# Removing the pauses inside the barrier norms of a two-layer hybrid encoder step

## The chip, the core and the metric

The kernel runs on one core of a Trainium2 chip. The metric is the device time of one execution in microseconds (us). The kernel before takes 2740.53 us, the median of three runs (2738.47 to 2742.73).

## What is computed

One inference step of a two-layer encoder over 640 positions: 512 of a new stream and 8 running streams of 16. Cut to what matters here, a layer is

```
h = rmsnorm(x, g_pre_mix);  u = h @ w_in
...   three branches (convolution, attention, state space) from u, merged by gates
x = x + rmsnorm(merged @ w_out, g_post_mix)
f = rmsnorm(x, g_pre_ffn) @ w_gate_up
f = (silu(f[..., :D_FF]) * f[..., D_FF:]) @ w_down
x = x + rmsnorm(f, g_post_ffn)
rmsnorm(x, g) = x * rsqrt(mean(x * x) + EPS) * g
```

The model width is 1024, the feed-forward width 2816. Two norms stand next to each other at each of a layer's two barriers: the norm after `w_out` or `w_down`, whose result is added to x, and the norm ahead of the next projection, which needs all 1024 channels of that x.

## The kernel before, in words

**Layout.** Activations lie transposed: 8 tiles of 128 channels by 640 positions. The positions are cut in two halves, half 0 of 256 and half 1 of 384 columns (`HALF`). A *unit* (`Unit`) is one 128x128-column strip of a weight matrix for all its inputs. Each weight and each activation is split in two parts (`split`: a rounded part on ScalarE, the rest on VectorE), and three matmuls per pair make up for the precision, so a unit with 8 input tiles is 24 matmuls per half. Its sum lies in a PSUM buffer of the pool `psg`, of which there are four (tile names `pg`). After the matmuls an evacuation function reads the buffer and frees it.

**A norm.** `sq_acc` (line 414) squares each evacuated tile on ScalarE (tile `sq`, the first of them `acc`) and VectorE adds it to `acc`. `colsum` (line 184) sums over the channels with matmuls against ones (tile `cs`), `rsqrt` (line 191) is nine small VectorE instructions (last one `ry`), `bcast` (line 208) spreads the root over 128 partitions with matmuls (tile `rb`). In `postnorm` (line 424) the eight tiles of x are loaded again (`xl`), VectorE multiplies the eight tiles by `rb` and gain and adds `xl`, `squares` (line 390) squares the eight results on ScalarE (`psq`) and adds them in seven steps on VectorE, and the results go to DRAM. `prenorm` (line 398) then takes `colsum`, `rsqrt`, `bcast` again, writes eight tiles `ht` on VectorE, and splits them into the parts `hh` (ScalarE) and `hl` (VectorE) that the next units read.

**Order of the work.** The code is written as one list of actions. `barrier` and `add_halves` (lines 336 and 325) write a stage's units like this: half 0 of all eight units of `w_out` (or `w_down`), then half 1 of all eight; beside half 1 runs the norm of half 0. Then come twelve units of the next stage with half 0, and beside them runs the norm of half 1; then the halves 1 of these. "Beside" is a generator: after each half unit, `pump` (line 283) gives each lane a credit, and one credit lets a norm be written up to its next `yield`. So the yields say after how many units which part of a norm is written into the program. In the units of 8 input tiles a lane gets one step per half unit, with a step saved up from before, so two after the first; in the 7-input units of `w_down` it gets 0.875.

**What written order decides.** The tile framework then places each instruction on the queue of its engine at build time: as early as what it needs is ready in the framework's own estimate, and among several that are ready the one that is written first. So written order is no order of execution. But each pool hands out its buffers strictly in the order in which the code first writes them. In the program of the kernel before, none of the 904 tiles of the pool `hf` is first written out of that order. `hf` (line 87) has 11 buffers, and `acc`, `sq`, `xl`, `psq`, `ht`, and the feed-forward evacuation's `ft` and `fg` all come from it.

**Evacuations.** `wout` (line 1301) copies the PSUM buffer and squares it from PSUM (`sq`), so the buffer is free after both. `down` (line 1337) adds the buffer to `dn` on VectorE and squares `dn`, so its buffer is free without an `hf` tile. `gu` (line 1322) writes, for a gate unit, tanh into `ft` (ScalarE), then `fg` (VectorE); for the up unit behind it `fg` is multiplied by the buffer and split. `ev_lora` (line 540) copies the buffer and squares it from PSUM into `acc` or `sq`.

Of the kernel before, what the change touches and what calls it, by code (L numbers as in the profile page):

```python
# [17 lines left out]
D_MODEL, SEQ, DEPTH, NB, DS, PAST = 1024, 512, 2, 8, 16, 256  # L18
# [53 lines left out]
BY = 2  # L72
# [4 lines left out]
def emit(tc, ctx, I, O):  # L77
# [27 lines left out]
    def hf(w, s="h", dt=F32):  # L105
        return hpool.tile([P, w], dt, tag="hf", name=nm(s))
# [7 lines left out]
    def tiny(shape, s="t", dt=F32):  # L114
        return tpool.tile(shape, dt, tag="t", name=nm(s))

    def psb(shape, s="pb"):
        return psb_.tile(shape, F32, tag="pb", name=nm(s))

    def mm(ps, l, r, a, b):  # L120
        nc.tensor.matmul(ps, l, r, start=a, stop=b)  # L121
# [14 lines left out]
    def tt(eng, o, a, b, op):  # L136
        eng.tensor_tensor(o, a, b, op=op)  # L137

    def stt(o, a, s, b, op0, op1):
        return V.scalar_tensor_tensor(o, a, s, b, op0=op0, op1=op1)  # L140
# [10 lines left out]
    def split(hi, lo, src, eng=None):  # L151
        nc.scalar.copy(hi, src)  # L152
        tt(eng or V, lo, src, hi.bitcast(F32), ALU.subtract)
# [30 lines left out]
    def colsum(sq, n):  # L184

        ps = psb([P, 24], "cs")
        for j in range(n):
            mm(ps[:, j:j + 1], sq[:, j * P:(j + 1) * P], C["ones"], True, True)
        return ps

    def rsqrt(ps, n, scale, post=1.0):

        v, q = ps[:, 8:8 + n], ps[:, 16:16 + n]
        s, r, t, y = (tiny([P, 8], x)[:, :n] for x in ("rs", "rr", "rt", "ry"))
        a = V.tensor_scalar(v, ps[:, :n], scale / post ** 2, EPS / post ** 2, op0=ALU.mult, op1=ALU.add)
        for i in tap.values():
            tc.add_manual_dep(a.ins, i.ins.name, behind)
        V.tensor_scalar(s.bitcast(I32), v.bitcast(I32), 0.5, float(0x1fbb4f2e), op0=ALU.mult, op1=ALU.add)
        V.reciprocal(r, s)
        tt(V, q, v, r, ALU.mult)  # L200
        tt(V, t, q, s, ALU.add)
        V.reciprocal(r, t)
        tt(V, q, v, r, ALU.mult)
        stt(t, t, 0.25 * HERON ** 2, q, ALU.mult, ALU.add)
        root.append(V.reciprocal(y, t))
        return y

    def bcast(y, n):
        rb = psb([P, n * P], "rb")
        for j in range(n):  # L210
            mm(rb[:, j * P:(j + 1) * P], y[:, j:j + 1].broadcast_to([P, P]), C["ident2"], True, True)
        return rb
# [144 lines left out]
    def layer(l):  # L357
# [21 lines left out]
        def par(n, j):  # L379
            o = _PK[n][0]  # L380
            return L["pk"][:, o + j:o + j + 1]


        def new_h():
            L["h"] = [tuple(blk([P, NT], t, F32R) for t in ("hh", "hl")) for _ in range(8)]
# [4 lines left out]
        def squares(xs, half):  # L390
            r = [hf(HW[half], "psq") for _ in range(8)]
            for k in range(8):
                act(r[k], xs[k][:, HALF[half]], AF.Square)
            for a, b in ((0, 1), (2, 3), (4, 5), (6, 7), (0, 2), (4, 6), (0, 4)):
                tt(V, r[a], r[a], r[b], ALU.add)
            return r[0]

        def prenorm(xs, sq, half, gname, ps=None):
            c, w, n = HALF[half], HW[half], HCH[half]
            if ps is None:  # L400
                ps = colsum(sq, n)
            yield
            y = rsqrt(ps, n, 1.0 / D_MODEL)
            yield
            rb = bcast(y, n)
            for k in range(8):
                tmp = hf(w, "ht")
                stt(tmp, xs[k][:, c], par(gname, k), rb, ALU.mult, ALU.mult)
                hh, hl = L["h"][k]
                split(hh[:, c], hl[:, c], tmp)  # L410
            yield
# [12 lines left out]
        def postnorm(key, tiles, half, gname, src, dst, sq=True):  # L424

            c, n, w = HALF[half], HCH[half], HW[half]
            yield
            ps = colsum(L.pop(("sq", key, half)), n)
            xs = []
            for k in range(8):  # L430
                xs.append(hf(w, "xl"))
                dma(xs[k], src[k][:, c])
            yield
            rb = bcast(rsqrt(ps, n, 1.0 / D_MODEL), n)
            for k in range(8):
                t = tiles[k][:, c]
                stt(t, t, par(gname, k), rb, ALU.mult, ALU.mult)
                tt(V, t, t, xs[k], ALU.add)
            r = squares(tiles, half) if sq else None
            for k in range(8):  # L440
                dma(dst[k][:, c], tiles[k][:, c])
            for _ in range(BY):
                yield
            return r


# [865 lines left out]
        def bar_mix(half):  # L1312
            sq = yield from postnorm("mo", L["mo"], half, "g_post_mix", xin, xd)
            if half == 0:
                new_h()
            yield
            yield from prenorm(L["mo"], sq, half, "g_pre_ffn")


# [34 lines left out]
        def bar_ffn(half):  # L1354
            sq = yield from postnorm("dn", L["dn"], half, "g_post_ffn", xd, O["y"] if last else xd, not last)
            if not last:
                nxt = layers[l + 1]
                if half == 0:
                    nxt["load_params"]()
                    nxt["new_h"]()  # L1360
                yield
                yield from nxt["prenorm"](L["dn"], sq, half, "g_pre_mix")

        def start():
# [3 lines left out]
        def first_norm(half):  # L1368
            sq = ps = None
            if half == 0:  # L1370

                ps = psb([P, 24], "cs")
                r = [hf(HW[0], "psq") for _ in range(8)]
                for k in range(8):
                    act(r[k], x0[k][:, HALF[0]], AF.Square)
                    if k % 2 == 0:
                        continue
                    tt(V, r[k], r[k], r[k - 1], ALU.add)
                    for j in range(HCH[0]):

                        mm(ps[:, j:j + 1], r[k][:, j * P:(j + 1) * P], C["ones"], k == 1 and j == 0, k == 7 and j == HCH[0] - 1)
            else:
                for _ in range(Y1):
                    yield
                sq = squares(x0, 1)
                yield
            yield from prenorm(x0, sq, half, "g_pre_mix", ps)

        def schedule():
# [36 lines left out]
            add_units([mix_ssm(m) for m in range(8)])  # L1426
            us = [u for j in range(6) for u in gu(j)]
            barrier([wout(m) for m in range(8)], KEEP_W[1], bar_mix, us[-KEEP_W[2]])
            add_halves(us, KEEP_W[2])
            for g in range(3):  # L1430
# [5 lines left out]
            if last:  # L1436

                add_halves([down(2, m) for m in range(8)], KEEP_W[3], 1, lambda: lanes["bar"].append(bar_ffn(1)))
                add_hook(lambda: lanes["bar2"].append(bar_ffn(0)))
                add_hook(lambda: (flush("bar"), flush("bar2")))  # L1440

        xin = I["x"] if l == 0 else xd
        return dict(schedule=schedule, start=start, load_params=load_params, new_h=new_h, prenorm=prenorm, bar_ffn=bar_ffn, down=down)

    layers = [layer(l) for l in range(DEPTH)]
# [181 lines left out]
```

## Time and profile before

| what | value |
|---|---|
| median of three runs | 2740.53 us |
| the profiled execution's own time | 2738.25 us |
| its span, first to last instruction | 2736.4 us |
| TensorE busy | 2647.6 us, 97% |
| VectorE, ScalarE, GpSimd busy | 1557.0, 1092.8, 810.7 us |
| mean granted TensorE clock | 0.988 |

TensorE's idle time is 88.8 us in all. The four barriers stand at 820 to 910 us (layer 0, `w_out`), 1310 to 1420 us (`w_down` of layer 0 into layer 1), 2195 to 2295 us (layer 1, `w_out`) and 2700 us to the end. Busy times of a stage say how full an engine is there; what a wait costs is read from TensorE's waits in that stage.

### The profile page before, as it was taken

The numbers are of one execution on the slowest core, as the hardware profiler recorded it, in microseconds if no ns is written. First come the engines' busy times: TensorE is split into PE (matmuls) and PEld (weight loads), VectorE is DVE, ScalarE is ACT, GpSimd is POOL, SyncE is SP. The second block draws the span as 40 slices with busy tenths as digits, with TensorE's granted clock in tenths as the row PEclk, the third lists the DMA queues.
The fourth block names the chain that finished last, engine by engine and source line by source line (L and its number), as shares of the span: only waits on it lengthen the run. The fifth ranks groups of instructions, "written<-read, shape, count | busy, mean of one in ns | idle before, by whom it ended". The sixth has DMA issues, their size and how long they took to land. (4 is left out here: it accounts for less than half of the span.)

```text
span 2736.4 us, 47467 instructions
## 1 busy us (share of the span) xinstructions
PE 2647.6 (97%) x17652; PEld 2556.6 (93%) x17652; DVE 1557.0 (57%) x3382; ACT 1092.8 (40%) x2437; POOL 810.7 (30%) x796
## 2 busy tenths in 40 slices
PE   7999999999999899999999899999999998999997
PEld 7999898889999899999999898989999998999997
DVE  6364759576566632333665648677656666323336
ACT  5535454434325432222445354544433344322222
POOL 5554555554420000000156544645544200000000
PEclk9999999999999999999999999999999999999999
DMA  6453244543734432222454432453436443222224
GB/s 185 147 159 102 75 135 111 156 131 119 239 121 137 149 93 74 70 82 72 139 166 158 129 98 87 128 143 120 145 110 230 133 159 120 86 77 70 78 74 131
DMA packets 248536, 337.81 MB, mean 123 GB/s; under 512 B 52464, under 2 KB 139056, under 8 KB 248304
## 3 DMA queue, kind: packets, MB, share of 16 engines
q1 hardware_dynamic: 246720, 333.75, 39.2%
q8 instruction: 139, 2.28, 0.3%
q10 hardware_dynamic: 1584, 1.02, 0.1%
q14 instruction: 93, 0.76, 0.1%
HBM read 268.73 MB, written 65.94 MB: 122 GB/s over the span
## 5 line engine op out<-in xcount | busy, mean ns | idle before, releaser
L121 PE MATMUL pg<-hh,wh 128*128 128x256 f32 (+1 forms) x3296 | 1048.4, 319 | 25.6 <-DVE fg L140 18.2
L121 PE MATMUL pg<-hl,wh 128*128 128x256 f32 (+1 forms) x3296 | 1035.1, 314 | 4.6 <-DVE hl L137 4.6
L121 PE MATMUL pg<-hh,wl 128*128 128x256 f32 (+1 forms) x3296 | 1029.2, 313 | 0.0
L137 POOL TENSOR_TENSOR wl<-raw,wh 128x512 fp32r<-128x512 f32 (+2 forms) x364 | 506.8, 1398 | 1158.5 <-ACT wh L152 1106.3
L152 ACT CAST wh<-raw 128x512 fp32r<-128x512 f32 (+1 forms) x696 | 423.7, 610 | 846.7 <-PE pg L121 737.9
L121 PEld LDWEIGHTS pg<-hh,wh 128*128 128x128 f32 x3296 | 627.3, 190 | 37.7 <-DVE fg L140 18.6
L121 PEld LDWEIGHTS pg<-hl,wh 128*128 128x128 f32 x3296 | 627.6, 191 | 13.8 <-DVE hl L137 5.3
L121 PEld LDWEIGHTS pg<-hh,wl 128*128 128x128 f32 x3296 | 627.0, 190 | 5.6 <-issue 3.9
L137 DVE TENSOR_TENSOR wl<-raw,wh 128x512 fp32r<-128x512 f32 x332 | 224.3, 677 | 338.6 <-ACT wh L152 337.0
L121 PE MATMUL pg<-fh,wh 128*128 128x256 f32 (+1 forms) x648 | 200.6, 310 | 0.0
L121 PE MATMUL pg<-fl,wh 128*128 128x256 f32 (+1 forms) x648 | 200.1, 309 | 0.0
L121 PE MATMUL pg<-fh,wl 128*128 128x256 f32 (+1 forms) x648 | 200.0, 309 | 0.0
L140 DVE SCALAR_TENSOR_TENSOR cv<-pp,pk,cv 128x512 f32<-128x512 f32 x184 | 158.8, 863 | 2.7 <-POOL cv L137 2.7
L121 PEld LDWEIGHTS pg<-fh,wh 128*128 128x128 f32 x648 | 122.0, 188 | 0.0
L121 PEld LDWEIGHTS pg<-fl,wh 128*128 128x128 f32 x648 | 122.0, 188 | 0.0
L121 PEld LDWEIGHTS pg<-fh,wl 128*128 128x128 f32 x648 | 121.9, 188 | 0.0
L140 DVE SCALAR_TENSOR_TENSOR sa<-pd,pk,sa 128x664 f32<-128x664 f32 x96 | 106.6, 1110 | 16.9 <-ACT sa L996 16.3
L137 POOL TENSOR_TENSOR cv<-cv,cvt 128x640 f32<-128x640 f32 x56 | 89.8, 1603 | 74.4 <-ACT cvt L907 66.2
L140 DVE SCALAR_TENSOR_TENSOR cv<-sp,pk,cv 128x128 f32<-128x128 f32 x184 | 94.8, 515 | 0.0
L137 DVE TENSOR_TENSOR fg<-fg,pg 128x256 f32<-128x256 f32 (+1 forms) x88 | 42.6, 486 | 83.5 <-PE pg L121 83.2
L152 ACT CAST fh<-fg 128x256 fp32r<-128x256 f32 (+1 forms) x88 | 40.3, 460 | 111.3 <-DVE fg L137 108.3
L137 DVE TENSOR_TENSOR acc<-acc,sq 128x256 f32<-128x256 f32 (+1 forms) x96 | 59.8, 625 | 37.4 <-ACT sq L421 35.9
(307 smaller groups left out, 4411.7 us busy)
## 6 DMA issues: line engine op xcount, KB each, us to landing
raw<-in_w_in SPq DMA_DIRECT2D x284, 256.0 KB, 2.9
raw<-in_w_gu SPq DMA_DIRECT2D x208, 256.0 KB, 2.7
raw<-in_w_down SPq DMA_DIRECT2D x72, 256.0 KB, 2.7
raw<-in_w_mix SPq DMA_DIRECT2D x64, 256.0 KB, 3.0
ma<-gd SPq DMA_DIRECT2D x48, 320.0 KB, 4.7
raw<-in_w_out SPq DMA_DIRECT2D x48, 256.0 KB, 2.7
gd<-gs SPq DMA_DIRECT2D x48, 192.0 KB, 2.2
hb<-in_state_ssm SPq DMA_DIRECT2D x64, 128.0 KB, 3.2
```

What stands on the lines that cost most here:

```text
L121: nc.tensor.matmul(ps, l, r, start=a, stop=b)
L137: eng.tensor_tensor(o, a, b, op=op)
L140: return V.scalar_tensor_tensor(o, a, s, b, op0=op0, op1=op1)
L152: nc.scalar.copy(hi, src)
```

## The change

In `prenorm` the two pauses between the column sums and the root and between the root and the broadcast go, in `postnorm` the one between the loads and the root; behind `postnorm` one pause is left of two, and the pause between the two norms goes at both kinds of barrier. The instructions, their number and their tiles stay as they are. With `BY = 2`, written steps per norm pair go from 8 to 3: one empty step, then everything of `postnorm`, then everything of `prenorm`.

```diff
@@ prenorm
             if ps is None:
                 ps = colsum(sq, n)
-            yield
-            y = rsqrt(ps, n, 1.0 / D_MODEL)
-            yield
-            rb = bcast(y, n)
+            rb = bcast(rsqrt(ps, n, 1.0 / D_MODEL), n)
             for k in range(8):
@@ postnorm
                 dma(xs[k], src[k][:, c])
-            yield
             rb = bcast(rsqrt(ps, n, 1.0 / D_MODEL), n)
@@ postnorm
                 dma(dst[k][:, c], tiles[k][:, c])
-            for _ in range(BY):
-                yield
+            yield
             return r
@@ bar_mix
                 new_h()
-            yield
             yield from prenorm(L["mo"], sq, half, "g_pre_ffn")
@@ bar_ffn
                     nxt["new_h"]()
-                yield
                 yield from nxt["prenorm"](L["dn"], sq, half, "g_pre_mix")
```

## Rows read from the trace of the kernel before

**Rows 1.** The page, part 1: busy time, share and instructions of each engine.
```profile
PE 2647.6 (97%) x17652; PEld 2556.6 (93%) x17652; DVE 1557.0 (57%) x3382; ACT 1092.8 (40%) x2437; POOL 810.7 (30%) x796
```

**Rows 2.** Busy time by stage: length, PE, PEld, DVE, ACT, POOL (instructions), clock, DMA.
```profile
820.00:910.00 90.00, 79.46 (x571) 79.06 (x570) 62.49 (x147) 44.45 (x99) 0.00 (x0) 0.96 0.52 167
910.00:1310.00 400.00, 400.00 (x2692) 400.00 (x2691) 156.14 (x291) 119.88 (x230) 0.00 (x0) 1.00 0.26 80
1310.00:1420.00 110.00, 103.48 (x727) 102.66 (x726) 82.50 (x195) 55.16 (x120) 41.65 (x31) 0.94 0.54 168
...
2195.00:2295.00 100.00, 89.47 (x627) 89.07 (x626) 74.16 (x181) 47.90 (x106) 0.00 (x0) 0.95 0.46 150
```

**Rows 3.** TensorE's waits, barriers one, two, three: waited for, total us, times, longest.
```profile
PE pg L121 <- DVE fg L140: 9.1, 1, 9.1
PE pg L121 <- DVE hl L137: 1.5, 1, 1.5
...
PE rb L121 <- DVE ry L205: 2.5, 1, 2.5
PE pg L121 <- ACT sq L421: 2.4, 1, 2.4
PE pg L121 <- DVE hl L137: 1.7, 1, 1.7
...
PE pg L121 <- DVE hl L137: 1.4, 1, 1.4
```

**Rows 4.** Timeline of the first barrier, TensorE: start, us, instruction [idle before, releaser].
```profile
870.81 0.50 PE L121 MATMUL cs<-c_ones,psq 128*128 128x1 f32 x4
...
877.23 0.60 PE L121 MATMUL rb<-c_ident,ry 128*128 128x128 f32 x4
...
909.45 0.58 PE L121 MATMUL pg<-hh,wh 128*128 128x256 f32 x1 [9.08 <-DVE fg L140]
```

**Rows 5.** Timeline of the first barrier, ScalarE.
```profile
862.99 1.32 ACT L393 ACTIVATE psq<-mo 128x256 f32<-128x256 f32 x4
864.21 0.86 ACT L421 ACTIVATE sq<-pg 128x384 f32<-128x384 f32 x2
...
905.15 2.17 ACT L393 ACTIVATE psq<-mo 128x384 f32<-128x384 f32 x5
907.22 0.63 ACT L1325 ACTIVATE ft<-pg 128x256 f32<-128x256 f32 x2
...
920.89 0.38 ACT L1325 ACTIVATE ft<-pg 128x256 f32<-128x256 f32 x1 [0.93 <-PE pg L121]
```

**Rows 6.** Timeline of the first barrier, VectorE.
```profile
873.37 0.17 DVE L205 RECIPROCAL ry<-rt 128x2 f32<-128x2 f32 x1
...
911.25 0.55 DVE L137 TENSOR_TENSOR psq<-psq,psq 128x384 f32<-128x384 f32 x1
...
922.60 4.29 DVE L140 SCALAR_TENSOR_TENSOR ht<-mo,pk,rb 128x384 f32<-128x384 f32 x8 [1.73 <-PE rb L121]
926.81 0.41 DVE L140 SCALAR_TENSOR_TENSOR fg<-ft,pg 128x256 f32<-128x256 f32 x1
```

**Rows 7.** Timeline of the second barrier, rows of TensorE, ScalarE and VectorE.
```profile
1365.70 1.28 PE L121 MATMUL cs<-c_ones,acc 128*128 128x1 f32 x6
...
1378.12 0.83 PE L121 MATMUL rb<-c_ident,ry 128*128 128x128 f32 x6
...
1390.25 1.35 ACT L393 ACTIVATE psq<-dn 128x384 f32<-128x384 f32 x3
1391.50 0.37 ACT L421 ACTIVATE sq<-pg 128x256 f32<-128x256 f32 x1
...
1395.02 1.65 DVE L137 TENSOR_TENSOR psq<-psq,psq 128x384 f32<-128x384 f32 x1
```

**Rows 8.** The chain that ended last, at the kernel's end: start, us, what.
```profile
2723.39 0.59 PE cs L121 x4
2725.91 0.85 PE rb L121 x4
```

## The prediction

> **What bounds the kernel now.** I read the page's engine table first. TensorE is busy 97% of the span [rows 1], so time can only be won where it waits, and is lost wherever a new wait is made. Next the busy time by stage: beside the gate and up units, 910 to 1310 us, TensorE is busy for the whole 400 us, while each of the first three barriers leaves it idle for 6.5 to 10.5 us [rows 2]. Then its waits there: 9.1 us for `fg` and 1.5 us for `hl` at the first barrier, 2.5, 2.4 and 1.7 us at the second, and at the third the same as at the first [rows 3]. The question is what ends these waits, and the timelines answer it.
>
> The 9.08 us wait begins at 909.45 - 9.08 = 900.37, after six of the twelve gate and up units, with all four PSUM buffers full [rows 4]. The third unit's gate should have been evacuated long before, but its `ft` runs at 907.22, straight behind the last of the eight `psq` [rows 5]. It stands there because the `psq` were written ahead of it and both take `hf` buffers, which go out in written order. The same pattern shows twice more: two `sq` at 864.21 straight behind the last `psq` of half 0 [rows 5], and a `sq` of the second barrier at 1391.50 behind its last `psq` [rows 7], which ends the 2.4 us wait. So the norm's place in the written order decides which evacuations must wait for it.
>
> **What the change does to that order.** No instruction is added or taken away. The chain sums, root, broadcast, products is placed by readiness, not by writing: in half 0 the sums run at 870.81 and the broadcast only at 877.23 [rows 4], though the root had ended at 873.54 (873.37 + 0.17 [rows 6]). I take it that the framework's own estimate put it there, so writing it earlier moves the sums nothing. What moves is who queues for `hf`. Before, the eight `psq` stand behind the second unit's evacuation and the eight `ht` behind the seventh's. After, the `psq` stand behind the first unit's and the `ht` behind the second's. All evacuations from the third unit on now get their `hf` buffer only after the `ht`, thus after the second root and its broadcast. The loads of `xl` and the stores keep their place on SP's queue behind the same weight loads; the next layer's parameters are written two steps earlier on ScalarE's queue, but nothing reads them before the second norm. I cost these at nothing; if `xl` came late, the stretch between `rb` and `psq` would grow by it.
>
> **First and third barrier, half 0 (w_out).** Here the buffer is freed by the copy and by `sq`. With `sq` of the third unit behind the `ht`, TensorE stops after six units. That is where the sums already stand, 870.81 + 0.50 = 871.31. The root then ends at 873.37 + 0.17 = 873.54 [rows 6], the broadcast takes 0.60 us [rows 4], and the seventh unit follows at about 874.2. `sq` is on ScalarE, ahead of the `hh`, and waits for no `ht` itself. The broadcast would have cost TensorE its time anyway, so 2.3 us are lost. `ht` and `hl` are finished some 3.7 us earlier (877.23 against about 873.6 for the broadcast), so the wait of 1.5 us for `hl` goes [rows 3]. Sum: +0.8 us.
>
> **First and third barrier, half 1 (beside gate and up units).** `ft` of the third unit is behind the `ht` now, and so is its `fg`, on VectorE. The seventh unit can start only after: the last `psq` addition, the second sums, root and broadcast, eight `ht`, one `fg`. The last addition ended at 911.25 + 0.55 = 911.8 [rows 6]; about 1.4 us of `fg` and `fl` no longer stand in between (an estimate: four pieces of some 0.4 us each, less overlap), and 0.8 us comes from above, so 911.2. From sums to the end of the broadcast with idle engines the end of the kernel shows 2725.91 + 0.85 - 2723.39 = 3.4 us for half 0 [rows 8]; half 1 has six matmuls in place of four, say 3.7. Eight `ht` take 4.29 us and `fg` 0.41 [rows 6]. Together 911.2 + 3.7 + 4.3 + 0.4 + 0.1 for hand-overs = 919.7, against 909.45: +10.2 us, half 0 included. Later units lose nothing more, since no norm work is left.
>
> That `fg` can't pass the `ht` I take from a row: `fg` starts at 926.81, right when eight `ht` end, though its `ft` was done at 921.27 [rows 5, 6]. The Trainium skill, PSUM — Partial Sum Buffer, section Engine vs sequencer instructions, says that the queues of ScalarE and VectorE are strictly first in, first out; by that rule the 4.3 us are owed in full, and the row agrees. Were `fg` placed ahead of the `ht`, the term would be 5.9.
>
> **Second barrier (w_down into the next layer).** In half 0 the buffer is freed by VectorE without `hf`, so no wait is added. But five of the eight `sq` of half 1 queue behind the `ht`, and the sums of half 1, which ran at 1365.70 [rows 7], come some 7 us later (an estimate: eight `ht` of 0.4 us and five additions of 0.55 us are now ahead of them). Part is regained, as the broadcast came 12.4 us after the sums [rows 7] and needs only 6.4 where VectorE is free (870.81 to 877.23 [rows 4]): I take 3 us late. The last `psq` addition then ends at 1395.02 + 1.65 + 3 = 1399.7 [rows 7]; sums to broadcast 3.4 us more: 1403.1. `sq` of the third unit waits for that, so the seventh unit starts there and not at 1391.50 + 0.37 = 1391.9: +11.2 us. The bounds are +6 (not late at all, and the last addition 2 us sooner) and +15 (7 us late).
>
> **Start and end.** The first norm of half 0 is written out in one go either way, and half 1 there shows no wait in its stretch; the last barrier's norm has no `psq` and no second norm. Both 0, bounds -1 and +3.
>
> **The sum.** 10.2 + 10.2 + 11.2 = +31.6 us. The profiled execution took 2738.25 us (2736.4 us of span and 1.85 around it), 2.3 below the median. So 2738.25 + 31.6 = 2769.9 for such an execution, and 2772 for a median. The clock is left out of the sum: the three barriers show 0.94 to 0.96 against 1.00 beside them [rows 2]. Longer waits can add 1 or 2 us at each.
>
> **The rivals.**
> - *It works as written: the norms come sooner, and the program is faster.* Place: the broadcasts, which ran up to 3.7 us behind their roots (873.54 against 877.23 [rows 4, 6]). If the pauses held them back, each first and third barrier gains 1.5 + 3.7, the second its 2.5 + 1.7 and the 2.4: 17 us in all, 2723. It decides if evacuations find `hf` buffers in spite of the order. For it: VectorE and ScalarE have slack in these stages [rows 2]. Against it: three places where an evacuation waits for the last `psq`. The Trainium skill, Perfetto Trace Analysis, section Optimization Strategy, advises making what the idle engine waits for start sooner; by that rule the change would win these 17 us. 12%.
> - *Slower, but `fg` passes the `ht`, and the second barrier regains all:* 5.9 + 5.9 + 6 = +18, 2758. For it: the eight `ht` and `fg` are placed within little of each other. 18%.
> - *Slower still: the clock and a stop of the sixth unit at the second barrier come on top:* 12 or 13 at each, +45 with 5 at the start, 2786. 12%.
> - *Nothing moves*, since readiness decides and not writing: 2740. Against it: the order of the buffers. 5%.
>
> **The numbers.** My forecast, 2772, has 53%. The slower cases lie between 2752 and 2790; outside are the faster one, the unmoved one and 3% of tails, so that is the range. A measurement can tell about 0.2%, 5.5 us, from no change. Faster 0.12, same 0.05, slower 0.83.
>
> **What would show it.** Right: in the first barrier `ft` of the third unit stands behind the broadcast of the second norm, the wait for `fg` is 17 to 20 us in place of 9.1, and a wait of some 2 us for `ry` stands after six half 1 units of `w_out`; at the second barrier a long wait for `sq` or `ry`. Wrong: the 9.1 us wait is shorter, or `ft` stands ahead of the `ht`.

## The result, and the profile after

The changed kernel takes 2771.68 us, the median of four runs (2769.65 to 2773.86), against 2741.55 us for the kernel before in the same comparison: a ratio of 1.0114, 95% interval 1.0099 to 1.0129. The forecast was slower, 2772, in 2752 to 2790. Its profiled span is 2767.8 us, 31.4 more than before.

First the page of the changed kernel, part 1. It answers to [rows 1].

```profile
PE 2649.3 (96%) x17652; PEld 2556.6 (92%) x17652; DVE 1550.5 (56%) x3382; ACT 1092.0 (39%) x2437; POOL 820.3 (30%) x796
```

The work is the same: as many instructions, 1.7 us more of TensorE's time. The other 29.7 of the 31.4 us are idle time of TensorE: 118.5 us (2767.8 - 2649.3) in place of 88.8. Next the busy times by stage, with the columns of [rows 2]:

```profile
820.00:910.00 90.00, 84.92 (x611) 84.42 (x609) 59.30 (x141) 42.98 (x94) 0.00 (x0) 0.99 0.47 148
910.00:930.00 20.00, 5.92 (x25) 5.60 (x26) 16.29 (x40) 7.31 (x17) 0.00 (x0) 0.50 0.37 128
...
1310.00:1420.00 110.00, 96.96 (x653) 96.01 (x652) 66.72 (x167) 47.41 (x100) 23.11 (x18) 0.92 0.47 144
...
2195.00:2295.00 100.00, 84.51 (x600) 83.99 (x599) 66.34 (x160) 45.36 (x100) 0.00 (x0) 0.93 0.48 156
```

From 910 to 930 us TensorE works 5.92 of 20 us, at a granted clock of 0.50, the lower of its two levels (1.2 of 2.4 GHz). TensorE's waits at the first barrier (the third has the same, with 12.0 in place of 11.0) and at the second, to be held against [rows 3]:

```profile
PE cs L121 <- DVE psq L137: 11.0, 1, 11.0
PE pg L121 <- DVE fg L140: 4.7, 1, 4.7
PE rb L121 <- DVE ry L205: 3.5, 2, 2.0
...
PE pg L121 <- ACT acc L415: 6.2, 1, 6.2
PE rb L121 <- DVE ry L205: 3.9, 3, 2.0
PE pg L121 <- DVE hl L137: 2.5, 1, 2.5
PE pg L121 <- ACT hh L152: 1.0, 1, 1.0
```

One wait of 9.1 us for `fg` has become three in a row: for `psq`, for `ry`, for `fg`. The timeline of the first barrier shows how they hang together, rows of TensorE, then ScalarE, then VectorE. They answer to [rows 4 to 6].

```profile
878.88 0.68 PE L121 MATMUL rb<-c_ident,ry 128*128 128x128 f32 x4 [1.48 <-DVE ry L205]
...
917.39 1.41 PE L121 MATMUL cs<-c_ones,psq 128*128 128x1 f32 x6 [10.99 <-DVE psq L137]
...
920.77 1.62 PE L121 MATMUL rb<-c_ident,ry 128*128 128x128 f32 x6 [1.97 <-DVE ry L205]
...
927.11 0.58 PE L121 MATMUL pg<-hh,wh 128*128 128x256 f32 x1 [4.71 <-DVE fg L140]
...
916.69 0.38 ACT L1319 ACTIVATE ft<-pg 128x256 f32<-128x256 f32 x1 [3.34 <-DVE psq L137]
...
914.23 3.02 DVE L137 TENSOR_TENSOR psq<-psq,psq 128x384 f32<-128x384 f32 x6
...
922.43 4.29 DVE L140 SCALAR_TENSOR_TENSOR ht<-mo,pk,rb 128x384 f32<-128x384 f32 x8 [1.81 <-PE rb L121]
926.64 0.41 DVE L140 SCALAR_TENSOR_TENSOR fg<-ft,pg 128x256 f32<-128x256 f32 x1
```

TensorE stops at 906.40, after six gate and up units with all four PSUM buffers full. The last `psq` addition ends at 917.25, and then sums, root, broadcast, eight `ht` and one `fg` follow one another, and TensorE has nothing else to do meanwhile. `ft` was done at 917.07, but its `fg` stands behind all eight `ht`. The Trainium skill, PSUM — Partial Sum Buffer, section Engine vs sequencer instructions, says that VectorE's queue is strictly first in, first out; the 9.6 us from 917.07 to 926.64 agree.

**Stage by stage.** To see which stage the time went into, I take the time between marks: the first matmul on `lat`, the first matmul of 384 columns on `mg` (`w_out`, half 1), the first matmul of the last `w_down` group, and the same in layer 1. The two spans of gate and up units count to barriers 1 and 3. A row is the change against the kernel before, in us; the last column is the whole span.

| kernel | start | mixer 0 | barrier 1 | barrier 2 | mixer 1 | barrier 3 | end | sum |
|---|---|---|---|---|---|---|---|---|
| forecast | 0 | 0 | +10.2 | +11.2 | 0 | +10.2 | 0 | +31.6 |
| changed | +1.3 | +4.7 | +10.7 | +8.6 | -5.2 | +10.6 | +0.7 | +31.4 |
| x1_after_own | -0.1 | +4.3 | +1.6 | +5.9 | -0.9 | +0.4 | +0.9 | +12.0 |
| x2_before_own | -0.4 | +7.1 | +1.5 | -1.5 | +3.1 | +0.2 | +0.8 | +10.7 |
| x3_moved | +0.4 | +5.8 | -1.2 | +1.5 | -0.9 | -1.3 | +1.1 | +5.5 |
| x4_post_pause | +1.8 | +7.7 | +9.0 | +12.5 | -1.5 | +7.7 | +0.9 | +38.1 |
| x5_ht_late | -0.4 | +6.5 | -1.7 | +0.4 | -0.6 | -3.3 | +0.7 | +1.5 |
| x6_after_own6 | +10.1 | +0.3 | +1.0 | +3.0 | +0.6 | +0.5 | +0.7 | +16.2 |
| x8_after_hf14 | +1.7 | +2.8 | +10.3 | +9.4 | +2.9 | +11.6 | +0.5 | +39.1 |
| x9_after_own6_pool | +11.0 | +9.1 | -0.1 | +2.6 | -4.3 | +1.0 | +0.9 | +20.2 |
| x10_ht_mid | +1.7 | +6.2 | +7.0 | +2.4 | -2.6 | +7.0 | +0.2 | +21.8 |
| x11_ht_later | +1.6 | +4.2 | +4.7 | +5.6 | -0.4 | +1.0 | +2.8 | +19.5 |
| x12_half1_early | +0.3 | +4.4 | +12.7 | +11.6 | -0.1 | +12.6 | +0.6 | +42.1 |
| x13_half0_early | +2.0 | +6.1 | +2.7 | +3.2 | +0.5 | -0.1 | +1.0 | +15.2 |

The two mixers hold nothing that was changed, and yet they move by -5 to +9 us from kernel to kernel. It is not that the framework placed them anew. In the changed kernel, x3, x4, x5, x8 and x10 to x13, the instructions of both mixers (8 us at either end left out) stand in the same order on TensorE, VectorE, ScalarE and GpSimd as in the kernel before; only x1, x2, x6 and x9 have another order on some engine. What differs is when they run. An example is TensorE's wait for one load, in the first mixer of the kernel before, then of the changed kernel:

```profile
PE qlp L121 <- DMA al<-in_w_ukt: 2.2, 1, 2.2
...
PE qlp L121 <- DMA al<-in_w_ukt: 5.6, 2, 4.3
```

That is 3.4 of the 4.7 us. Each kernel has one profiled execution, and the kernel before alone took 2729.64 to 2752.41 us in thirteen executions of one comparison. Whether such a shift belongs to a kernel or to an execution is open. So a barrier is judged by its own columns, and a few us of a total say nothing.

### The profile page after: what moved, and what is told of

The parts are those of the page before. It is cut to its first block, busy times and chain, and to the rows that moved or that the text cites. A ratio compares the mean times of both kernels' runs of the same rounds, so it can differ in the third digit from the quotient of the medians.

```text
span 2767.8 us, 47456 instructions
## 1 busy us (share of the span) xinstructions
PE 2649.3 (96%) x17652; PEld 2556.6 (92%) x17652; DVE 1550.5 (56%) x3382; ACT 1092.0 (39%) x2437; POOL 820.3 (30%) x796
## 5 line engine op out<-in xcount | busy, mean ns | idle before, releaser
L137 POOL TENSOR_TENSOR wl<-raw,wh 128x512 fp32r<-128x512 f32 (+2 forms) x364 | 513.3, 1417 | 1159.8 <-ACT wh L152 1101.5
L121 PEld LDWEIGHTS pg<-hl,wh 128*128 128x128 f32 x3296 | 628.3, 191 | 11.6 <-issue 5.3
L140 DVE SCALAR_TENSOR_TENSOR sa<-pd,pk,sa 128x664 f32<-128x664 f32 x96 | 108.5, 1130 | 12.3 <-ACT sa L991 11.6
L121 PE MATMUL pg<-ynh,wl 128*128 128x256 f32 (+1 forms) x256 | 78.8, 309 | 0.0
```

## The experiments

**Do the evacuations wait because buffers go out in written order?** x1 gives them a pool of their own in the changed kernel, x2 in the kernel before (`ef` is `hf` on the new pool; its definition is left out).

```diff
@@ pools
     hpool = pool("hf", 11)
+    epool = pool("ef", 3)
@@ sq_acc
-                sq = hf(w, "sq")
+                sq = ef(w, "sq")
@@ gu
-            t, f = hf(HW[half], "ft"), hf(HW[half], "fg")
+            t, f = ef(HW[half], "ft"), ef(HW[half], "fg")
```

> The changed kernel, with the evacuations' ft, fg and sq in a pool of their own of 3 buffers; psq, ht, xl and acc stay in hf (11). Theory A (the loss comes from hf buffers being handed out in written order, so that evacuations queue behind psq and ht): at the first and third barriers the gap of about 20 us after six gate and up units goes; what is left there is the norm itself being late for the half 1 units, 5 to 8 us, so each is some 3 us shorter than in the kernel before. The second barrier still has acc and ga in hf and keeps most of its +8.6. Sum: 2741.5 - 3 - 3 + 8.6 + 1.3 = about 2745, 2735 to 2752. Theory B (the norm's instructions, written sooner, stand ahead of the evacuations on VectorE and ScalarE whatever the buffers): about 2771, with the waits for psq, ry and fg as in the changed kernel.

> The kernel before with the same own pool of 3 buffers for ft, fg and sq. Theory A: the 9.1 us wait for fg at the first and third barriers and the 2.4 us wait for sq at the second go; the half 1 norm is then late for the half 1 units by some 5 us at the first and third, so 4 us are won at each and 1 to 2 at the second: about 2732, 2725 to 2738. Theory B: 2741, unchanged, with the 9.1 us waits.

x1 takes 2750.21 us against 2742.86 (1.0024, 1.0015 to 1.0034), x2 2747.78 (1.0012, 0.9999 to 1.0025). Barriers 1 and 3 of x1 cost 1.6 and 0.4 where the changed kernel has 10.7 and 10.6: the loss there goes with the shared pool. Barrier 2 keeps +5.9, and there `acc` and `ga` still come from `hf`. But x2 wins nothing, against theory A's number, and x1's barriers 1 and 3 are not the 3 us shorter than before that it had. x1's waits at the first barrier, and rows of VectorE:

```profile
PE pg L125 <- DVE hl L141: 3.8, 2, 2.0
PE rb L125 <- DVE ry L209: 3.4, 1, 3.4
PE pg L125 <- ACT hh L156: 1.3, 1, 1.3
...
915.08 0.70 DVE L141 TENSOR_TENSOR wl<-raw,wh 128x512 fp32r<-128x512 f32 x1
...
917.69 0.43 DVE L141 TENSOR_TENSOR fg<-fg,pg 128x256 f32<-128x256 f32 x1
...
921.76 0.57 DVE L141 TENSOR_TENSOR psq<-psq,psq 128x384 f32<-128x384 f32 x1
...
929.77 4.29 DVE L144 SCALAR_TENSOR_TENSOR ht<-mo,pk,rb 128x384 f32<-128x384 f32 x8 [1.80 <-PE rb L125]
```

The wait for `fg` is gone. Evacuations and weight remainders now stand between the `psq` additions on VectorE, the last addition ends at 922.33, and TensorE waits at the end of its twelve units for the norm instead: 3.4, 1.3 and 1.9 us, 6.6 in all (the other 1.8 for `hl` stand ahead of the twelve units, where the kernel before has its 1.5). x2 has the same rows:

```profile
PE pg L125 <- DVE hl L141: 3.8, 2, 1.9
PE rb L125 <- DVE ry L209: 3.4, 1, 3.4
PE pg L125 <- ACT hh L156: 1.3, 1, 1.3
```

So with evacuations in a pool of their own the missing pauses change nothing at the first and third barriers: x1 and x2 stand at 1.6 and 1.5, and at 0.4 and 0.2. That is the strongest evidence that the shared pool is the only way by which the change acts there. Nor were the 9.1 us of the kernel before a loss that this pool wins back. In x2, between the marks of barrier 1, TensorE is idle for 8.8 us in place of 10.5, but busy for 459.5 in place of 456.2 with the same matmuls: either the units or the norm wait.

**Order, or too few buffers?** x8 is the changed kernel with `hpool = pool("hf", 14)` in place of 11.

> The changed kernel with 14 buffers in hf in place of 11, and nothing else. Theory A, order: buffers are still handed out in written order, so ft and fg of the third unit stay behind ht: 2770, 2763 to 2776, with waits for psq and fg at the first and third barriers. Rival, number: three free buffers let ft and fg go ahead: 2741 to 2752.

2776.48 us against 2743.89 (1.0115, 1.0095 to 1.0134), half a us above theory A's range, and at the first barrier the changed kernel's three waits:

```profile
PE cs L121 <- DVE psq L137: 10.7, 1, 10.7
PE pg L121 <- DVE fg L140: 4.7, 1, 4.7
PE rb L121 <- DVE ry L205: 3.5, 2, 2.0
```

It is the order. Three more buffers change nothing, while x1's three, handed out apart, take some 21 us off.

**The pauses themselves, or the place?** x3 is the kernel before with the two pauses inside `prenorm` moved ahead of it; x5 is the changed kernel with five pauses put between its two norms (and two at the start, which the cut leaves out).

```diff
@@ x3_moved, prenorm
-            yield
-            y = rsqrt(ps, n, 1.0 / D_MODEL)
-            yield
-            rb = bcast(y, n)
+            rb = bcast(rsqrt(ps, n, 1.0 / D_MODEL), n)
@@ x3_moved, ahead of each prenorm
+            yield
+            yield
@@ x5_ht_late, bar_mix and bar_ffn
+            for _ in range(5):
+                yield
             yield from prenorm(L["mo"], sq, half, "g_pre_ffn")
```

> The kernel before with the pauses between sums and root and between root and broadcast taken out of prenorm and as many put ahead of it: sums, root, broadcast and normed values are written in one go, but no earlier than before. Theory A (it is the place of psq and ht in the written order that costs): the buffers are handed out nearly as before, so 2741, 2736 to 2746, with the 9.1 us waits for fg and none of 11 us for psq. Theory C (that sums, root and broadcast are written without pauses costs by itself): part or all of the 30 us, 2755 to 2771.

> The changed kernel with five pauses ahead of prenorm at the barriers (two at the start): psq is written where the change puts it, ht where the kernel before had it. Theory A (an evacuation written behind ht is placed behind ht): the waits at the first and third barriers are those of the kernel before to 2 us, the second costs 0 to 3; with the layer 0 mixer 0 to 8 us longer, as the four runs had it, 2744, 2737 to 2752. Rival (psq written early costs too, the two places share the 30 us): 2755 to 2765.

x3 takes 2740.57 us (0.9989, 0.9980 to 0.9999), x5 2740.05 (0.9990, 0.9980 to 1.0001). In time both are what the kernel before is. So writing sums, root, broadcast and normed values in one go costs nothing, and neither does the early `psq`, nor the dropped pause behind the loads. The place of `prenorm`, from its sums to its `ht`, carries the whole 30 us; that `ht` is what counts in it is inferred from x1 and x2, since `ht` are the only tiles of `prenorm` in `hf`.

The waits are not those of the kernel before, though both expectations had them so. x3's at the first barrier, and half 0's sums:

```profile
PE cs L121 <- DVE acc L137: 2.7, 1, 2.7
PE pg L121 <- DVE fg L140: 2.6, 1, 2.6
PE pg L121 <- ACT hh L152: 1.2, 1, 1.2
...
881.29 0.50 PE L121 MATMUL cs<-c_ones,psq 128*128 128x1 f32 x4
```

x5 has 2.9 for `fg`, 2.7 for `acc` and 1.1 for `hh`. These sums, written two steps later in x3, run 30.4 us after the mark of the stage (881.29 - 850.94), against 26.1 in the kernel before (870.81 - 844.68). So the written order can delay the sums.

**Which half?** x12 keeps x5's five pauses for half 0 alone, x13 for half 1 alone (`range(0 if half else 5)` and the reverse).

> As x5_ht_late, with the five pauses for half 0 alone: half 1's ht are written where the change puts them. By the prediction's split, half 0 costs 0.8 us and half 1 the rest at each of the first and third barriers: 2767, 2760 to 2775, with waits of some 10 us for psq and 4.7 for fg there. By theory E, formed after x10_ht_mid (there the second sums of the first barrier ran at 896.48 with the first wait 11.2 us long, against 890.88 and 2.9 in x5_ht_late): half 0's early ht hold back the squares of half 1's w_out units, so half 1's sums come some 6 us late, and half 1's early ht cost only the remaining 5: 2752 to 2758.

> As x5_ht_late, with the five pauses for half 1 alone: half 0's ht are written where the change puts them. By the prediction's split: 2740 to 2745, the first and third barriers within 2 us of x5_ht_late. By theory E: the second sums of the first barrier run some 6 us later against the stage's start than in x5_ht_late, the first and third barriers cost about 5 to 7 each, the second 2: 2752 to 2760.

x12 takes 2780.78 us against 2741.36 (1.0145, 1.0129 to 1.0160), x13 2750.25 (1.0032, 1.0016 to 1.0049). TensorE's waits at the first barrier, rows of x12, then of x13:

```profile
PE cs L121 <- DVE psq L137: 7.0, 1, 7.0
PE pg L121 <- DVE fg L140: 4.7, 1, 4.7
...
PE rb L121 <- DVE ry L205: 2.0, 1, 2.0
...
PE pg L121 <- DVE fg L140: 9.4, 1, 9.4
PE rb L121 <- DVE ry L205: 1.5, 1, 1.5
```

The three waits in a row come with half 1's early `ht`: +12.7, +11.6, +12.6. Half 0's alone leave the old wait for `fg` (9.4) and cost +2.7, +3.2, -0.1. So half 1 carries the loss, as the prediction split it, but neither time lies in a range that was stated: x12 is 6 us above the prediction's, x13 5 above the prediction's and 2 below theory E's. Nor do the halves add up, since x12's half 1 alone costs more than the changed kernel's 10.7, 8.6 and 10.6. The rows do not bear out theory E's mechanism either. Half 1's sums run 3.6 us later in x13 than in x5 against each kernel's own mark of that stage (896.42 - 852.72 = 43.7, 890.88 - 850.78 = 40.1). But x5's are the early ones: in the kernel before, the last of these sums run at 43.5 too (888.20 - 844.68), and in the changed kernel, with half 0's `ht` as early as in x13, at 41.6 (892.22 - 850.67). The rows, of x5 and then of the kernel before:

```profile
890.88 1.41 PE L121 MATMUL cs<-c_ones,acc 128*128 128x1 f32 x6 [2.71 <-DVE acc L137]
...
888.20 0.28 PE L121 MATMUL cs<-c_ones,acc 128*128 128x1 f32 x2
```

**How much later is enough?** x4 gives `postnorm` its pause back; x10 and x11 have three and seven pauses where x5 has five.

```diff
@@ x4_post_pause, postnorm
+            yield
             rb = bcast(rsqrt(ps, n, 1.0 / D_MODEL), n)
@@ x10_ht_mid
-            for _ in range(5):
+            for _ in range(3):
```

> The changed kernel with the one pause of postnorm back (between the loads and the root): psq is written where it was before, and ht one unit later than in the changed kernel, still behind no pause of prenorm. Theory A: the third unit's ft and fg are written ahead of the ht now and the fifth's behind, so TensorE gets two more units before it stops; of the 10.7 us at the first and third barriers some 5 are left at each, and 5 of 8.6 at the second: about 2741.5 + 5 + 5 + 5 + 1.3 = 2758, 2750 to 2764. Theory C (the pauses inside prenorm are what counts): 2771, as the changed kernel.

> As x5_ht_late, but three pauses ahead of prenorm at the barriers in place of five: two gate units beyond the first pair's are written ahead of ht, the next behind. Theory A: TensorE can run ten of the twelve units before it needs an evacuation that stands behind ht; the two that are left run while hh and hl are made. So the cost has a threshold rather than a slope: 0 to 4 at the first and third barriers, 2745, 2738 to 2753. Rival (each unit of earlier writing costs its share of the 30 us): with two of five pauses missing 2753 to 2760.

> As x5_ht_late, but seven pauses in place of five. Theory A: no evacuation that TensorE needs stands behind ht in either, and ht is placed as soon as it is ready, so nothing moves: 2740, 2735 to 2747. Rival (the place sets the time in this direction as well, and ht comes late for the half 1 units): 2748 to 2755.

All three miss theory A's ranges; x10 lies in its rival's. x4 takes 2775.05 us (1.0108, 1.0093 to 1.0123), x10 2757.88 against 2742.61 (1.0054, 1.0039 to 1.0069), x11 2758.32 (1.0057, 1.0041 to 1.0074). In x4 TensorE does get two units more after the `psq` (919.85 to 924.68), but the second sums stand behind 26 of their 48 matmuls in its queue, at 924.52. Against the stage's mark that is 70.4 us, and 66.7 in the changed kernel (917.39 - 850.67): of two units won, 3.7 us are given back, and half 0's `ht` were moved too. x10 shows no threshold: barriers 1 and 3 cost 7.0 each. x11's losses lie in barriers 1 and 2 and at the end; what causes them is open. Open is also a rule for how far back `ht` should stand: 0, 3, 5, 7 pauses gave +30, +15, -4, +16 us (differences of medians, the -4 within the noise).

**Can a version beat both?** x6 takes x1's pool for the first six pairs alone and moves the low-rank branches' `acc` to `blk`; x9 also puts the weights' remainders of `w_out` and of these pairs on GpSimd.

> The changed kernel with ft and fg of the first six gate and up pairs and all sq in the own pool of 3, and the acc of the low-rank branches in blk: at the second barrier only ga and what follows are still written behind ht. Theory A: the +5.9 us that x1_after_own kept at the second barrier go to about -1; the first and third stay as there. 2744, 2738 to 2749. Rival (the second barrier is late because its norm is written later than the units, whatever the buffers): 2750.

> x6_after_own6 with the weights' remainders wl and wbl of w_out and of the first six gate and up pairs subtracted on GpSimd, which does nothing in that stage, instead of on VectorE. If VectorE's queue is what delays the second norm once the evacuations are free (14 remainders of 0.65 to 0.69 us stand among its work from 903 to 927 us in x1_after_own), the norm ends 6 to 9 us sooner and TensorE's 8.5 us of waits at the first and third barriers shrink by 5 each: 2733, 2725 to 2740. Rival: GpSimd takes 1.4 us for a remainder, two to a unit of 2.84 us, and TensorE waits for wl: 2745 to 2765.

No. x6 takes 2753.36 us against 2743.89 (1.0036, 1.0022 to 1.0050): barrier 2 falls from 5.9 to 3.0, where theory A had -1, and the start costs 10.1. `sq` came from the second pool in x1 as well, whose start stands at -0.1, so this goes with `acc` in `blk`. What holds the other 4 us at barrier 2 was not followed further. x9 takes 2758.82 (1.0054, 1.0038 to 1.0070). Its first and third barriers stand at -0.1 and +1.0, against x6's +1.0 and +0.5, where 5 us less each were forecast; what it loses to x6 lies in the first mixer (+9.1 against +0.3). TensorE's waits for `fg` (3.8 us) and `psq` (3.6) at the first barrier are none for `wl`, so the rival's reason is not there, though the time lies in its range. A reason for the missing gain is in groups of VectorE around the first barrier, two of the kernel before and then the same of x9:

```profile
L140 DVE SCALAR_TENSOR_TENSOR mo<-mo,pk,rb 128x256 f32<-128x256 f32 (+1 forms) x16 | 7.5, 540 | 1.9 <-PE rb L121 1.9
L137 DVE TENSOR_TENSOR mo<-mo,xl 128x256 f32<-128x256 f32 (+1 forms) x16 | 7.0, 483 | 0.0
...
L141 DVE TENSOR_TENSOR mo<-mo,xl 128x256 f32<-128x256 f32 (+1 forms) x16 | 12.3, 829 | 0.0
...
L144 DVE SCALAR_TENSOR_TENSOR mo<-mo,pk,rb 128x256 f32<-128x256 f32 (+1 forms) x16 | 7.5, 542 | 0.9 <-PE rb L125 0.9
```

The additions take 829 ns each in place of 483 (482 in x6), while GpSimd is at work: some 5.5 us more for the sixteen. x3 and x5 stand within 0.2% of the kernel before; nothing tried is clearly faster than it.

## Why the prediction was right, and where it was not

- **The buffer order.** Right, and shown by x1 against x8 and x2: the pool matters, its size doesn't. That writing the sums earlier moves them nothing is shown by the changed kernel, where half 0's run 25.8 us after the mark (876.45 - 850.67) and 26.1 before. It holds in that direction only, as x3's 30.4 shows.
- **First and third barrier.** +10.2 was forecast, +10.7 and +10.6 measured. By its steps: the last addition at 911.2, moved by the 6.0 us that the stage starts later, makes 917.2; it ended at 917.25. From there to the end of the broadcast 3.7 us were forecast and 5.1 measured (922.39): TensorE had stood idle for 11 us and, at the granted clock of 0.50, did the six sums in 1.41 us and the broadcast in 1.62, where the same shapes took 0.73 and 0.83 at the second barrier (rows below). This is the clock that the prediction left out of its sum. `ht` and `fg` took 4.29 and 0.41, as read. So the restart came 11.7 us late (927.11 - 909.45 - 6.0) and not 10.2; behind it 1 us was won back, and the mark after the barrier shows 10.7.
- **Half 0.** The wait for `ry` stands after six half 1 units of `w_out`, 1.48 us, and the wait for `hl` is gone, as forecast. +0.8 was forecast; half 0 alone (x13) costs 2.7 and -0.1.
- **A step that was wrong.** "`ft` of the third unit stands behind the broadcast": it ran at 916.69, ahead of it, as soon as `psq` buffers came free. Only `fg` stands behind `ht`. The price did not change, since the buffer is freed by `fg`. The one wait of 17 to 20 us came as three, 10.99 + 1.97 + 4.71 = 17.7, because sums and broadcast stand on TensorE's own queue between them. So by their letter both signs of being wrong that the prediction named came true: the wait put down to `fg` is shorter than 9.1, and `ft` stands ahead of the `ht`. The stop and what ends it are as forecast; the step that every evacuation from the third unit on gets its `hf` buffer only after the `ht` is not.
- **Second barrier.** +11.2 was forecast, +8.6 measured, and the step that failed is the end of the last addition, with a second one partly against it. Rows of the changed kernel, TensorE, ScalarE, VectorE:

```profile
1392.59 0.73 PE L121 MATMUL cs<-c_ones,acc 128*128 128x1 f32 x6
1397.91 0.83 PE L121 MATMUL rb<-c_ident,ry 128*128 128x128 f32 x6
...
1408.83 0.58 PE L121 MATMUL pg<-hh,wh 128*128 128x256 f32 x1 [6.16 <-ACT acc L415]
...
1413.88 0.72 PE L121 MATMUL cs<-c_ones,psq 128*128 128x1 f32 x6
1416.57 1.25 PE L121 MATMUL rb<-c_ident,ry 128*128 128x128 f32 x6 [1.97 <-DVE ry L205]
1417.48 0.56 PE L121 MATMUL pg<-hh,wh 128*128 128x256 f32 x1
...
1408.41 0.36 ACT L415 ACTIVATE acc<-pg 128x256 f32<-128x256 f32 x1
...
1407.87 3.48 DVE L137 TENSOR_TENSOR psq<-psq,psq 128x384 f32<-128x384 f32 x7
```

  The stage starts 16.7 us later than before. So the broadcast is 1397.91 - 1378.12 - 16.7 = 3.1 us late, the 3 that were taken [rows 7]. But the additions end at 1411.35, 2.0 us sooner than before and not 3 later, since no evacuation stands between them any more: VectorE does products, sums and squares in one stretch. That is the lower bound's "last addition 2 us sooner", and 5 us less than the forecast had. But TensorE stopped a unit earlier than forecast, behind `acc`, and the second sums stand behind the sixth unit in its queue. So from the last addition to the end of the broadcast 3.4 us were forecast and 6.5 measured (1417.82 - 1411.35), 3.1 more. The seventh unit starts behind the broadcast, as forecast, at 1417.48: 8.9 us late (1417.48 - 1391.9 - 16.7) and not 11.2.
- **Start.** 0 was forecast; +1.3 measured, with a new wait:

```profile
46.51 0.39 PE L121 MATMUL pg<-hh,wh 128*128 128x256 f32 x1 [2.30 <-ACT acc L415]
```

  `acc` of a low-rank unit is written behind the norm's `ht` there too; x5, with two pauses ahead of that norm, has no such wait. The +1.3 lie within the bounds given.
- **The mixers.** Not in the sum: +4.7 and -5.2. They nearly cancel, and so do the 2.6 us too many for barrier 2 and the 2.9 too few for the start, the end and barriers 1 and 3. So the nearness of 2771.68 to 2772 is partly luck; the three barriers alone, 29.9 against 31.6, are the fair measure. Why the kernel before has the shortest layer 0 mixer of all fourteen kernels was not tried.
- **The rivals.** The faster one rested on advice of the Trainium skill, Perfetto Trace Analysis, section Optimization Strategy, to start sooner what the idle engine waits for. The norm was written sooner, and its last addition in the first barrier ended only 0.5 us sooner (917.25 - 6.0 = 911.3, before 911.8): that is not what the rule asks for, since TensorE waited for `fg`, and the change made the norm sooner and put `fg` behind it. The rival with `fg` ahead of the `ht` is ruled out by the rows of the first barrier (`ht` at 922.43, `fg` at 926.64). The slower rival's stop of the sixth unit at the second barrier did come, without its price.

## What to carry to other kernels

Where a framework hands out a pool's buffers in written order, the place at which a long block of work is written decides which short, urgent work stands behind it, even if both are placed by readiness. Look for an evacuation that runs straight behind a block it has nothing to do with, and test it with a second pool before changing sizes: the number of buffers is another question. And a wait that such a pool takes away may only have hidden the next one.

## What the runs showed of the hardware

With GpSimd subtracting remainders (54 of some 1.33 us each in x9 between 820 and 945 us), VectorE's additions of two tensors in SBUF in the same stretch took 829 ns on the mean for `mo` against 483 in the kernel before (820 to 930 us), and 602 against 482 for `psq` (x6, without GpSimd's part, has 482 and 483); its products with `rb`, which lies in PSUM, stayed at 542 against 540. So work moved to an idle engine was paid for on the busy one, by some of its operations alone. The Trainium skill, SBUF — State Buffer, section 🔬 SBUF: two separate sides, says that VectorE and GpSimd share a pair of ports, held by one of them for a whole instruction, and that VectorE needs the pair for an operation with two inputs in SBUF, against a GpSimd operation that reads SBUF. The additions and the products agree.
